# A two-layer hybrid trunk in fp32r: VectorE put in program order, weight tiles split two tiles ahead

## The chip, the cores and the metric

The kernel runs on one core of a Trainium2 chip. The metric is device microseconds of one execution. The kernel before took 2461.07 us (median of three runs, 2458.48 to 2471.07).

## The reference

Two decoder layers over 256 tokens of width 2048, in float32. Layer 0 mixes tokens with stick-breaking attention, layer 1 with an S5 state-space layer and a gated linear unit (GLU). After each mixer stands a dense MLP of width 8192.

```
cond = silu(c)
for i in range(2):
    sh1, sc1, g1, sh2, sc2, g2 = split(cond @ ada_w[i] + ada_b[i], 6)   # the conditioning vectors
    h = rmsnorm(x, ln1_g[i]) * (1 + sc1) + sh1
    y = stick_breaking_mixer(h) if i == 0 else s5_mixer(h)
    x = x + g1 * y
    h = rmsnorm(x, ln2_g[i]) * (1 + sc2) + sh2
    a = relu(h @ mlp_w1[i])
    x = x + g2 * ((a * a) @ mlp_w2[i])
```

`s5_mixer` is `u = h @ w_in`, a scan over time in 16 blocks of 128 channels, `z = gelu(y + d * u)`, and `(z @ w_glu)` cut in two halves `a * sigmoid(g)`.

## The kernel before

All weights stream from HBM, one pass: 736 weight tiles `w` of 512 KB (`weights`, L126). Each product is made of three matmuls on rounded halves, so each weight tile is rounded by ScalarE to `wh` (L131) and the rest `wl = w - wh` is made by VectorE (L133). `w`, `wh` and `wl` have three buffers each. TensorE then runs 24 matmuls of about 256 columns on a tile (L160 to L162, `cols_tile`), or 12 of 512 columns (L146 to L148, `gemm_rows`). The tiles come in this order: attention 0 to 127, first MLP 128 to 383, S5 input product 384 to 415, GLU 416 to 479, second MLP 480 to 735.

Beside them runs a second stream, the conditioning vectors. `ada_w` comes in 384 loads of 512 KB (`adaw`, four buffers, L268 and L270). From the first MLP on one such load is one product on VectorE (L354, L356) into one of three accumulators (`adsums`, two buffers, and `adacc`); after 16 loads an accumulator is full, and after 32 TensorE sums it over partitions (`totals`, L327). One call of `tick` stands behind each weight tile. It lets `pump` emit `rate` loads of this stream (1.0 for the first 16 tiles of the first MLP, 0.42 in the rest of it, 0.35 in S5), plays three recorded VectorE operations of S5's tables (`Recorder`, L35), and runs what was planned for this tick. In the GLU `pace(44, ...)` sets the rate so that the vectors `mid` are done by the sixth of its eight groups, where `drain` asks for them and `fold` makes the operands `hH`, `hL` of the second MLP.

What sets the order: TensorE and GpSimd run in the order of the program's text. VectorE, ScalarE and the queue of SyncE (SP), which issues nearly all loads, are ordered by a scheduler that takes what it believes to be ready, by priority. So a conditioning product could stand ahead of its place in the text, until all three accumulators were taken.

S5 in one block `bi` of 128 channels, by ticks: `s5_windows` (VectorE L1029, ScalarE L1030) makes `u` from the product; a tick later `s5_shuffle` (TensorE L1038) gathers `u` through the identity; a tick after that `s5_states` runs eight matmuls of L1053 per complex half and seven VectorE operations (L1055 to L1063); four ticks later `s5_outputs` (L1078, L1079) makes `y`. The next block's `s5_windows` is in the same tick as this block's `s5_states`, and stands behind it in the text.

Of the kernel before, what the change touches and what calls it, by code (L numbers as in the profile page):

```python
# [8 lines left out]
F32 = mybir.dt.float32  # L9
# [3 lines left out]
AF = mybir.ActivationFunctionType  # L13
OP = mybir.AluOpType
AX = mybir.AxisListType

P = 128
D = 2048
NB = D // P
# [37 lines left out]
class Trunk:  # L57
    def __init__(self, ctx, tc, ins, out, dbg=None):
        self.ctx, self.tc, self.nc = ctx, tc, tc.nc
        self.i, self.out, self.dbg = ins, out, dbg or {}  # L60
        self.pers = ctx.enter_context(tc.tile_pool(name="pers", bufs=1))
        self.wp = ctx.enter_context(tc.tile_pool(name="wp", bufs=1))
        self.ps = ctx.enter_context(tc.tile_pool(name="ps", bufs=1, space=bass.MemoryType.PSUM))
        self.queue = []
        self.acc2 = self.wp.tile([P, 2, 512], F32, name="adacc", bufs=1)


# [55 lines left out]
        self.nc.vector.tensor_tensor(lo, src, hi.bitcast(F32), op=OP.subtract)  # L123


    def weights(self, src, a, b):  # L126
        nc = self.nc
        w = self.wp.tile([P, a, b], F32, name="w", bufs=self.nw)
        nc.sync.dma_start(w, src)
        h = self.wp.tile([P, a, b], F32R, name="wh", bufs=self.nh)  # L130
        nc.scalar.activation(h, w, AF.Copy)  # L131
        l = self.wp.tile([P, a, b], F32R, name="wl", bufs=self.nh)
        nc.vector.tensor_tensor(l, w, h.bitcast(F32), op=OP.subtract)  # L133
        return h, l

    def gemm_rows(self, w2d, c0, aH, aL, k0, k1):
        nc = self.nc
        acc = self.accs()
        for t in range(k0 // 2, k1 // 2):
            r0 = 2 * t * P  # L140
            H, L = self.weights(w2d[r0:r0 + 2 * P, c0:c0 + 512].rearrange("(a p) b -> p a b", p=P), 2, 512)
            for kk in range(2):
                kb = 2 * t + kk
                for tb in range(2):
                    o, s = acc[:, tb], slice(tb * P, tb * P + P)
                    nc.tensor.matmul(o, aL(kb)[:, s], H[:, kk], start=(kb == k0), stop=False)  # L146
                    nc.tensor.matmul(o, aH(kb)[:, s], L[:, kk], start=False, stop=False)  # L147
                    nc.tensor.matmul(o, aH(kb)[:, s], H[:, kk], start=False, stop=(kb == k1 - 1))  # L148
            self.tick()
        return acc  # L150

    def cols_tile(self, acc, w2d, c0, t, aH, aL, k0=0, k1=NB):
        nc = self.nc
        r0, n = 4 * t * P, aH(0).shape[-1]
        H, L = self.weights(w2d[r0:r0 + 4 * P, c0:c0 + 256].rearrange("(a p) b -> p a b", p=P), 4, 256)
        for kk in range(4):
            kb = 4 * t + kk
            for j in range(2):
                o, s = acc[:, j, :n], slice(j * P, j * P + P)
                nc.tensor.matmul(o, L[:, kk, s], aH(kb), start=(kb == k0), stop=False)  # L160
                nc.tensor.matmul(o, H[:, kk, s], aL(kb), start=False, stop=False)  # L161
                nc.tensor.matmul(o, H[:, kk, s], aH(kb), start=False, stop=(kb == k1 - 1))  # L162
        self.tick()
# [155 lines left out]
    def ada_dve(self, layer, groups):  # L319
        nc = self.nc  # L320
        st, rows = {}, 32 * len(groups)

        def totals(i0, accs):
            if i0 == 0:
                st["bank"] = self.ada_bank()
            for i, acc in enumerate(accs, i0):
                nc.tensor.matmul(st["bank"][32 * i:32 * i + 32], self.ones[:, 0:32], acc, start=True, stop=True)  # L327

        def evict():
            st["sm"] = self.ada_sums(st["bank"], rows)  # L330

        def finish():
            p2 = self.mp()
            for b in range(4):
                nc.tensor.transpose(p2[:, b * P:b * P + rows], st["sm"][:rows, b * P:b * P + P], self.ident[:rows, :rows])
            src = p2.rearrange("p (b i r) -> p i r b", b=4, i=4)[:, :, 0]
            for i, (vec, g) in enumerate(groups):
                self.ada_done(layer, vec, 4 * g, 4, src[:, i])

        accs = []  # L340
        if self.sums is not None:
            for i in range(0, len(groups), 2):
                if self.turn % 3:
                    acc = self.sums.tile([P, 1024], F32, name="adsums", bufs=2)
                else:
                    acc = self.acc2.rearrange("p a b -> p (a b)")
                self.turn += 1
                accs += [acc[:, :512], acc[:, 512:]]
                vec, g = groups[i]
                for k in range(NB):  # L350
                    wt = self.ada_load(layer, vec, g, k, wide=True).rearrange("p a b -> p (a b)")
                    c = self.cond[:, k:k + 1]
                    if k == 0:
                        nc.vector.tensor_scalar(acc, wt, c, None, op0=OP.mult)  # L354
                    else:
                        nc.vector.scalar_tensor_tensor(acc, wt, c, acc, op0=OP.mult, op1=OP.add)  # L356
                    yield
            self.later(2, totals, 0, accs)
        for i, (vec, g) in enumerate(groups if not accs else []):
            acc = self.acc2[:, self.turn % 2]  # L360
            self.turn += 1
            accs.append(acc)
            for t in range(8):
                wt = self.ada_load(layer, vec, g, t)
                for kk in range(2):
                    c = self.cond[:, 2 * t + kk:2 * t + kk + 1]
                    if t + kk == 0:
                        nc.vector.tensor_scalar(acc, wt[:, kk], c, None, op0=OP.mult)
                    else:
                        nc.vector.scalar_tensor_tensor(acc, wt[:, kk], c, acc, op0=OP.mult, op1=OP.add)  # L370
                yield
            self.later(2, totals, i, accs[i:])
        self.later(2, evict)
        self.later(3, finish)

    def ada_vec(self, layer, vec, on_pe=False):
        g = self.pending[layer, vec] = self.ada(layer, [(vec, g) for g in range(4)], on_pe)
# [61 lines left out]
    def square(self, sq, kb):  # L439
        nc = self.nc  # L440
        if kb == 0:
            nc.scalar.activation(sq, self.xT[:, kb], AF.Square)
        else:
            t = self.wp.tile([P, S], F32, name="sqt", bufs=2)
            nc.scalar.activation(t, self.xT[:, kb], AF.Square)
            nc.vector.tensor_tensor(sq, sq, t, op=OP.add)

    def new_sq(self):
        return self.wp.tile([P, S], F32, name="sqa", bufs=1)
# [52 lines left out]
    def mlp(ctx, self, layer, nxt=None, last=False, between=None):  # L502
        nc = self.nc
        w1, w2 = self.i["mlp_w1"][layer], self.i["mlp_w2"][layer]
# [3 lines left out]
        sq = self.new_sq() if nxt else None  # L508
# [3 lines left out]
        for q in range(4):  # L512
            aH = rp.tile([P, NB, S], F32R, name="aH", bufs=1)
            aL = rp.tile([P, NB, S], F32R, name="aL", bufs=1)
            if q == 0:
# [3 lines left out]
                for g in range(ahead):  # L519
                    acc = self.gemm_cols(w1, g * 256, hH, hL, 0, 8)  # L520
# [4 lines left out]
            for g in range(8):  # L525
                if 8 * q + g < ahead:
                    acc = self.gemm_cols(w1, q * 2048 + g * 256, hH, hL, 8, 16)
                    r = src = halves[8 * q + g]
                    nc.vector.tensor_tensor(src, src, acc[:, :, :S + 1], op=OP.add)
                else:  # L530
                    src = self.gemm_cols(w1, q * 2048 + g * 256, hH, hL)
                    r = rp.tile([P, 2, S + 1], F32, name="rl")
                self.normal(r, src, AF.Relu)
                r = r[:, :, :S]
                nc.scalar.activation(r, r, AF.Square)
                self.split(aH[:, 2 * g:2 * g + 2], aL[:, 2 * g:2 * g + 2], r)
            if q == 3 and nxt:
                nxt()
                self.sq = sq
            if last:  # L540
                for g in range(4):
                    c = slice(g * 512, g * 512 + 512)
                    acc = self.gemm_rows(w2[q * 2048:q * 2048 + 2048], g * 512, lambda kb: aH[:, kb], lambda kb: aL[:, kb], 0, NB)
# [14 lines left out]
            for g in range(8):  # L558
                acc = self.gemm_cols(w2[q * 2048:q * 2048 + 2048], g * 256, lambda kb: aH[:, kb], lambda kb: aL[:, kb])[:, :, :S]
# [4 lines left out]
                if q == 1 and between:  # L564
                    nc.vector.tensor_tensor(halves[g], halves[g], acc, op=OP.add)
                    acc = halves[g]
# [616 lines left out]
    def run(self):  # L1183
        nc = self.nc
# [28 lines left out]
        self.modulate(0, 4)  # L1213
        self.attention(sets, gates[0])
        self.dump("x1")
        M = lambda i: bool(0 >> i & 1)
        self.sums = self.ctx.enter_context(self.tc.tile_pool(name="sums", bufs=1))
        mid = [self.ada_vec(1, 4, M(4)), self.ada_vec(1, 3, M(5))]
        nxt = [self.ada_vec(1, 1, M(1)), self.ada_vec(1, 0, M(2))]
# [64 lines left out]
```

## Time and profile before

| | |
|---|---|
| median of the runs | 2461.07 us |
| the profiled execution's own time | 2467.97 us |
| its span | 2466.1 us |
| TensorE matmul busy | 2365.1 us, 96% of the span |
| VectorE busy | 1795.4 us, 73% |
| ScalarE busy | 1212.7 us, 49% |
| moved by DMA | 627.09 MB, 254 GB/s over the span |
| mean granted TensorE clock | 0.989 |

Matmuls overlap, so their busy time hides part of what is lost between them; the count of matmuls in a stretch tells more. The shares are means over stages of different kinds, so the stretches in the rows below are cut along the stages: 572 to 1306 us is most of the first MLP, 1347 to 1498 us is S5, 1539 to 1673 us most of the GLU, and from 1719 us on the second MLP runs.

### The profile page before, as it was taken

To read this page: it belongs to the slowest core of one execution; us is meant where nothing else is said; L and a number is where in the kernel's file an instruction comes from. 1 tells how busy PE (TensorE), PEld (TensorE's weight loads), DVE (VectorE), ACT (ScalarE), POOL (GpSimd) and SP (SyncE) were. 2 spreads that over 40 slices of the span, in tenths; PEclk is the share of its full clock that TensorE was granted. 3 is DMA by queue.
4 is the path that set the end of the run, shared out by engine and by line. 5 is a ranking of instruction groups with operands and counts; after the bars stand their busy time and mean duration, and the time that the engine had idled before them with its cause. 6 is when DMAs were issued, how large, how long until landed. Compare 5 with 4: busy or idle time off the path is not lost.

```text
span 2466.1 us, 45235 instructions
## 1 busy us (share of the span) xinstructions
PE 2365.1 (96%) x18355; PEld 2160.4 (88%) x18355; DVE 1795.4 (73%) x2223; ACT 1212.7 (49%) x1814; POOL 316.6 (13%) x340
## 2 busy tenths in 40 slices
PE   7999999999998999889999999989999999999999
PEld 4777789899988899889998998989998998998987
DVE  5789999999778767875786668888744554555554
ACT  4534875346334335435546776434554543543543
POOL 0000110001056545445300000000000000000000
PEclk9999999999999999999999999999999999999999
DMA  9888899999999967997798544999856555556565
GB/s 341 302 299 306 288 308 320 322 303 294 310 310 315 300 207 230 309 299 219 259 316 276 174 154 159 314 329 314 281 175 192 184 186 190 175 179 193 180 195 164
DMA packets 416773, 627.09 MB, mean 254 GB/s; under 512 B 19858, under 2 KB 282420, under 8 KB 414260
## 3 DMA queue, kind: packets, MB, share of 16 engines
q1 hardware_dynamic: 411968, 606.16, 74.8%
q0 software_dynamic: 3968, 17.83, 2.2%
q8 instruction: 144, 2.36, 0.4%
q14 instruction: 65, 0.53, 0.1%
q10 hardware_dynamic: 628, 0.21, 0.0%
HBM read 607.34 MB, written 16.78 MB: 253 GB/s over the span
## 4 chain that ended last, share of the span: by engine, by line
PE 44%; DMA 6%; DVE 5%; issue 3%; ACT 0%; SPq 0%; DVEq 0%; ACTq 0%
PE acc L160 9%; PE acc L162 8%; PE acc L161 8%; DMA adaw<-in_ada_w 5%; PE acc L146 5%; PE acc L148 5%; PE acc L147 5%; DVE wl L133 2%; PE mp L1053 1%; DVE adsums L356 1%; PE mp L1078 1%; PE mp L1038 1%; PE mp L1015 1%; DVE xT L435 1%; DMA w<-in_s_w_glu 0%
## 5 line engine op out<-in xcount | busy, mean ns | idle before, releaser
L131 ACT ACTIVATE wh<-w 128x1024 fp32r<-128x1024 f32 x736 | 777.5, 1058 | 1030.9 <-PE acc L162 364.6
L133 DVE TENSOR_TENSOR wl<-w,wh 128x1024 fp32r<-128x1024 f32 x736 | 922.6, 1255 | 436.9 <-ACT wh L131 434.3
L160 PE MATMUL acc<-hH,wl 128*128 128x258 f32 (+1 forms) x2816 | 808.4, 287 | 28.4 <-DVE wl L133 26.1
L162 PE MATMUL acc<-hH,wh 128*128 128x258 f32 (+1 forms) x2816 | 799.2, 284 | 0.0
L161 PE MATMUL acc<-hL,wh 128*128 128x258 f32 (+1 forms) x2816 | 797.8, 283 | 0.2 <-DVE hL L123 0.2
L160 PEld LDWEIGHTS acc<-hH,wl 128*128 128x128 f32 x2816 | 535.8, 190 | 44.3 <-DVE wl L133 33.6
L161 PEld LDWEIGHTS acc<-hL,wh 128*128 128x128 f32 x2816 | 536.3, 190 | 0.6 <-DVE hL L123 0.4
L162 PEld LDWEIGHTS acc<-hH,wh 128*128 128x128 f32 x2816 | 534.8, 190 | 0.0
L160 PE MATMUL acc<-aH,wl 128*128 128x256 f32 x1024 | 294.3, 287 | 26.4 <-DVE wl L133 25.5
L161 PE MATMUL acc<-aL,wh 128*128 128x256 f32 x1024 | 289.5, 283 | 0.0
L162 PE MATMUL acc<-aH,wh 128*128 128x256 f32 x1024 | 289.4, 283 | 0.0
L356 DVE SCALAR_TENSOR_TENSOR adsums<-adaw,cond,adsums 128x1024 f32<-128x1024 f32 x150 | 199.1, 1328 | 53.6 <-DMA adaw<-in_ada_w 53.0
L160 PEld LDWEIGHTS acc<-aH,wl 128*128 128x128 f32 x1024 | 194.3, 190 | 34.1 <-DVE wl L133 33.7
L146 PE MATMUL acc<-wh,aL 128*128 128x512 f32 x512 | 202.2, 395 | 0.0
L148 PE MATMUL acc<-wh,aH 128*128 128x512 f32 x512 | 202.1, 395 | 0.0
L147 PE MATMUL acc<-wl,aH 128*128 128x512 f32 x512 | 202.0, 395 | 0.0
L161 PEld LDWEIGHTS acc<-aL,wh 128*128 128x128 f32 x1024 | 194.4, 190 | 0.0
L162 PEld LDWEIGHTS acc<-aH,wh 128*128 128x128 f32 x1024 | 194.2, 190 | 0.0
L370 DVE SCALAR_TENSOR_TENSOR adacc<-adaw,cond,adacc 128x512 f32<-128x512 f32 x240 | 179.2, 750 | 3.1 <-DMA adaw<-in_ada_w 1.3
L146 PE MATMUL acc<-wh,hL 128*128 128x512 f32 x384 | 157.5, 410 | 5.8 <-ACT wh L131 3.1
L147 PE MATMUL acc<-wl,hH 128*128 128x512 f32 x384 | 153.8, 401 | 3.3 <-DVE wl L133 3.2
L148 PE MATMUL acc<-wh,hH 128*128 128x512 f32 x384 | 152.9, 398 | 0.0
(311 smaller groups left out, 2751.0 us busy)
## 6 DMA issues: line engine op xcount, KB each, us to landing
w<-in_mlp_w SPq DMA_DIRECT2D x512, 512.0 KB, 4.0
adaw<-in_ada_w SPq DMA_DIRECT2D x384, 512.0 KB, 6.0
w<-in_sb_w_in SPq DMA_DIRECT2D x96, 512.0 KB, 5.2
w<-in_s_w_glu SPq DMA_DIRECT2D x64, 512.0 KB, 5.4
w<-in_sb_w_out SPq DMA_DIRECT2D x32, 512.0 KB, 5.7
w<-in_s_w_in SPq DMA_DIRECT2D x32, 512.0 KB, 4.8
pw<-W POOLq DMA_DIRECT2D x8, 1024.0 KB, 6.5
W<-pw SPq DMA_DIRECT2D x8, 1024.0 KB, 7.7
```

Source lines behind the costliest of these rows:

```text
L131: nc.scalar.activation(h, w, AF.Copy)
L133: nc.vector.tensor_tensor(l, w, h.bitcast(F32), op=OP.subtract)
L146: nc.tensor.matmul(o, aL(kb)[:, s], H[:, kk], start=(kb == k0), stop=False)
L147: nc.tensor.matmul(o, aH(kb)[:, s], L[:, kk], start=False, stop=False)
L148: nc.tensor.matmul(o, aH(kb)[:, s], H[:, kk], start=False, stop=(kb == k1 - 1))
L160: nc.tensor.matmul(o, L[:, kk, s], aH(kb), start=(kb == k0), stop=False)
L161: nc.tensor.matmul(o, H[:, kk, s], aL(kb), start=False, stop=False)
L162: nc.tensor.matmul(o, H[:, kk, s], aH(kb), start=False, stop=(kb == k1 - 1))
L356: nc.vector.scalar_tensor_tensor(acc, wt, c, acc, op0=OP.mult, op1=OP.add)
L370: nc.vector.scalar_tensor_tensor(acc, wt[:, kk], c, acc, op0=OP.mult, op1=OP.add)
L435: nc.vector.scalar_tensor_tensor(x, y, self.mod[layer][:, vec * 16 + kb:vec * 16 + kb + 1], x, op0=OP.mult, op1=OP.add)
L1015: nc.tensor.transpose(pe[:, q * P:q * P + P], E[:, c, q].rearrange("p j a e -> p (j a e)"), self.ident)
```

## The change

From the first MLP on VectorE is in program order too (`manual_schedule` with DVE). Four things in the text change with it:

- `weights` no longer loads and splits the tile that is asked for; it keeps three tiles ready. A generator lists the tiles in the order of use, and the load, the rounding and the split of tile t+2 stand ahead of the matmuls of tile t.
- A conditioning product is emitted when the load two places behind it has been emitted (`overdue(2)`), and all that are left ahead of `totals`.
- The split of the MLP's activations (`aL`) and the sum of squares are put off by one tick (`behind`).
- All else on VectorE keeps its place in the text, and so gets that place on the engine.

```diff
-        self.queue = []
+        self.queue, self.seq, self.ready, self.due = [], None, [], []
...
     def weights(self, src, a, b):
+        if self.seq is None:
+            return self.fetch(src, a, b)
+        while len(self.ready) < 3 and self.seq:
+            nxt, a_, b_ = self.seq.pop(0)
+            self.ready.append((str(nxt), self.fetch(nxt, a_, b_)))
+        name, pair = self.ready.pop(0)
+        assert name == str(src), (name, str(src))
+        return pair
+
+    def fetch(self, src, a, b):
+        src = src.rearrange("(a p) b -> p a b", p=P)
         nc = self.nc
         w = self.wp.tile([P, a, b], F32, name="w", bufs=self.nw)
         nc.sync.dma_start(w, src)
...
         def totals(i0, accs):
+            self.overdue(0)
...
-                    c = self.cond[:, k:k + 1]
-                    if k == 0:
-                        nc.vector.tensor_scalar(acc, wt, c, None, op0=OP.mult)
-                    else:
-                        nc.vector.scalar_tensor_tensor(acc, wt, c, acc, op0=OP.mult, op1=OP.add)
+                    self.due.append((self.ada_product, acc, wt, k))
+                    self.overdue(2)
...
+    def overdue(self, n):
+        while len(self.due) > n:
+            fn, *args = self.due.pop(0)
+            fn(*args)
...
-            nc.vector.tensor_tensor(sq, sq, t, op=OP.add)
+            self.behind(nc.vector.tensor_tensor, sq, sq, t, OP.add)
+
+    def behind(self, fn, *args):
+        if self.seq is None:
+            fn(*args)
+        else:
+            self.at(1, fn, *args)
...
-                self.split(aH[:, 2 * g:2 * g + 2], aL[:, 2 * g:2 * g + 2], r)
+                nc.scalar.activation(aH[:, 2 * g:2 * g + 2], r, AF.Copy)
+                self.behind(nc.vector.tensor_tensor, aL[:, 2 * g:2 * g + 2], r, aH[:, 2 * g:2 * g + 2].bitcast(F32), OP.subtract)
...
         self.dump("x1")
+        self.ctx.enter_context(self.tc.manual_schedule(engines={mybir.EngineType.PE, mybir.EngineType.Pool, mybir.EngineType.DVE}))
+        self.seq = list(self.tiles())
```

Place one is SP's queue in the first MLP, from weight tile 236 on (`w` a weight tile, `adaw` a conditioning load). The kernel before:

```order
L129 DMA w<-in_mlp_w 128x4x256 x2
L268 DMA adaw<-in_ada_w 128x1024
L129 DMA w<-in_mlp_w 128x4x256
L268 DMA adaw<-in_ada_w 128x1024
L129 DMA w<-in_mlp_w 128x4x256 x42
L268 DMA adaw<-in_ada_w 128x1024
L129 DMA w<-in_mlp_w 128x4x256
L268 DMA adaw<-in_ada_w 128x1024 x2
```

And the changed kernel in the same stage:

```order
L165 DMA w<-in_mlp_w 128x4x256 x2
L304 DMA adaw<-in_ada_w 128x1024
L165 DMA w<-in_mlp_w 128x4x256 x3
L304 DMA adaw<-in_ada_w 128x1024
L165 DMA w<-in_mlp_w 128x4x256 x2
L304 DMA adaw<-in_ada_w 128x1024
```

Before, conditioning loads come close together and then stop for 42 weight tiles; now one stands behind every two or three weight tiles all along.

Place two is SP's queue in the GLU, from about weight tile 424 on. The kernel before:

```order
L129 DMA w<-in_s_w_glu 128x4x256 x2
L268 DMA adaw<-in_ada_w 128x1024
L129 DMA w<-in_s_w_glu 128x4x256 x2
L268 DMA adaw<-in_ada_w 128x1024
L129 DMA w<-in_s_w_glu 128x4x256
L268 DMA adaw<-in_ada_w 128x1024
```

And the changed kernel:

```order
L304 DMA adaw<-in_ada_w 128x1024 x3
L165 DMA w<-in_s_w_glu 128x4x256 x2
L304 DMA adaw<-in_ada_w 128x1024 x2
L165 DMA w<-in_s_w_glu 128x4x256
L304 DMA adaw<-in_ada_w 128x1024 x2
L165 DMA w<-in_s_w_glu 128x4x256
```

Counted along the whole queue, from weight tile 424 to 464 there stood 45 conditioning loads before and there stand 62 now. Up to tile 424 there were 308 of them before and are 290 now, and up to tile 464 the counts meet, 353 and 352.

Place three is VectorE in S5, one block of 128 channels (`u` the window, `w` and `R` the state's products, `M` the scan's factors). The kernel before:

```order
L1079 SCALAR_TENSOR_TENSOR u_14061<-u_14061,colv,mp 128x4x64
L1055 TENSOR_TENSOR w_14863<-mp,T 128x512
L1056 TENSOR_TENSOR w_14864<-mp,T 128x512
L1029 TENSOR_TENSOR u_14061<-acc,rms 128x257
L1057 TENSOR_TENSOR R<-w_14863,w_14864 128x512
L1060 SCALAR_TENSOR_TENSOR R<-M_14064,R 128x512
L1061 TENSOR_TENSOR w_14863<-R,T 128x512
L1062 TENSOR_TENSOR w_14864<-R,T 128x512
L133 TENSOR_TENSOR wl<-w,wh 128x1024
L1063 TENSOR_TENSOR R<-w_14863,w_14864 128x512
```

And the changed kernel (L1132 was L1079, L1108 to L1116 were L1055 to L1063, L1082 was L1029):

```order
L1132 SCALAR_TENSOR_TENSOR u_14070<-u_14070,colv,mp 128x4x64
L1108 TENSOR_TENSOR w_14685<-mp,T 128x512
L1109 TENSOR_TENSOR w_14686<-mp,T 128x512
L1110 TENSOR_TENSOR R<-w_14685,w_14686 128x512
L1113 SCALAR_TENSOR_TENSOR R<-M_14073,R 128x512
L1114 TENSOR_TENSOR w_14685<-R,T 128x512
L1115 TENSOR_TENSOR w_14686<-R,T 128x512
L1116 TENSOR_TENSOR R<-w_14685,w_14686 128x512
L1082 TENSOR_TENSOR u_14070<-acc,rms 128x257
L169 TENSOR_TENSOR wl<-w,wh 128x1024
```

The window `u` stood behind the second of the seven state operations and stands behind the seventh now; so it does in 15 of the 16 blocks. TensorE's and GpSimd's order is the same in both kernels.

## Rows read from the trace of the kernel before

**Rows 1.** Busy time by stretch; columns as the first line says, (x) counts instructions.
```profile
core 0: us, PE busy (x) PEld busy (x) DVE busy (x) ACT busy (x) POOL busy (x), PEclk, DMA share, GB/s
572.00:870.00 298.00, 274.74 (x2195) 268.25 (x2194) 244.25 (x234) 129.58 (x161) 119.64 (x116) 0.98 0.91 303
870.00:960.00 90.00, 90.00 (x758) 90.00 (x757) 57.74 (x63) 40.82 (x49) 35.92 (x42) 1.00 0.69 208
960.00:1120.00 160.00, 145.93 (x1190) 141.54 (x1189) 128.53 (x126) 62.61 (x72) 86.45 (x82) 1.00 0.88 291
1120.00:1200.00 80.00, 80.00 (x670) 80.00 (x670) 49.06 (x47) 42.45 (x55) 40.44 (x44) 1.00 0.74 227
1200.00:1306.00 106.00, 103.81 (x863) 101.81 (x862) 92.98 (x113) 51.62 (x74) 0.00 (x0) 1.00 0.90 300
1347.00:1498.00 151.00, 150.47 (x2596) 138.35 (x2595) 104.33 (x144) 110.40 (x231) 0.00 (x0) 1.00 0.51 160
1539.00:1673.00 134.00, 122.10 (x988) 118.04 (x987) 113.35 (x131) 53.82 (x69) 0.00 (x0) 0.99 0.94 323
1560.00:1620.00 60.00, 55.28 (x456) 53.42 (x455) 52.18 (x66) 25.87 (x35) 0.00 (x0) 1.00 0.98 339
1740.00:1800.00 60.00, 60.00 (x504) 60.00 (x503) 44.57 (x42) 33.59 (x46) 0.00 (x0) 1.00 0.82 267
```

**Rows 2.** Who waited for whom, 572 to 1306 us: total us, times, longest.
```profile
ACT wh L131 <- DMA w<-in_mlp_w: 221.9, 108, 5.6
...
PEld acc L160 <- DVE wl L133: 50.3, 48, 3.4
PE acc L160 <- DVE wl L133: 38.6, 36, 3.2
```

**Rows 3.** DMA issues, 572 to 870 us: count, size, median us to landing.
```profile
w<-in_mlp_w SPq DMA_DIRECT2D x90, 512.0 KB, 5.4
adaw<-in_ada_w SPq DMA_DIRECT2D x67, 512.0 KB, 6.1
```

**Rows 4.** DMA issues, 870 to 960 us.
```profile
w<-in_mlp_w SPq DMA_DIRECT2D x31, 512.0 KB, 3.8
```

**Rows 5.** VectorE by line, 554 to 590 us: busy us, mean ns, idle before.
```profile
L133 DVE TENSOR_TENSOR wl<-w,wh 128x1024 fp32r<-128x1024 f32 x12 | 14.5, 1218 | 1.1 <-ACT wh L131 1.1
L356 DVE SCALAR_TENSOR_TENSOR adsums<-adaw,cond,adsums 128x1024 f32<-128x1024 f32 x7 | 9.0, 1281 | 1.4 <-DMA adaw<-in_ada_w 1.4
L497 DVE TENSOR_TENSOR half<-half,rms 128x514 f32<-128x514 f32 x6 | 4.1, 686 | 0.0
```

**Rows 6.** VectorE's table operations (L35), 494 to 620 us: busy us and count.
```profile
494.00:620.00 126.00, 17.46 (x76) 1.00 0.91 301
```

**Rows 7.** The folds (L484): shortest, median and longest ns.
```profile
L484 DVE SCALAR_TENSOR_TENSOR hL<-xT,mod,hH x48: 476/479/483, 433.7 to 1726.7; 128x256 fp32r<-128x256 f32 x48
```

**Rows 8.** One S5 block in order of time: start us, duration us.
```profile
1409.14 0.69 DVE L1055 TENSOR_TENSOR w<-mp,T 128x512 f32<-128x512 f32 x1 [0.66 <-PE mp L1053]
...
1410.35 0.42 DVE L1029 TENSOR_TENSOR u<-acc,rms 128x257 f32<-128x257 f32 x1
1410.68 0.68 DVE L1057 TENSOR_TENSOR R<-w,w 128x512 f32<-128x512 f32 x1
1410.80 0.51 ACT L1030 ACTIVATE u<-u 128x256 f32<-128x256 f32 x1 [1.42 <-DVE u L1029]
...
1413.55 1.13 PE L1038 MATMUL mp<-u,ident 128*32 128x65 f32 x32
1413.87 1.22 DVE L133 TENSOR_TENSOR wl<-w,wh 128x1024 fp32r<-128x1024 f32 x1
...
1415.00 0.68 DVE L1063 TENSOR_TENSOR R<-w,w 128x512 f32<-128x512 f32 x1
```

**Rows 9.** DMA of the GLU, 1539 to 1673 us: GB/s in 40 slices, then issues.
```profile
GB/s 285 311 278 304 285 208 221 350 221 380 359 268 391 329 304 373 382 374 353 377 357 295 359 367 360 376 368 379 375 376 379 378 248 162 320 251 270 235 363 357
...
adaw<-in_ada_w SPq DMA_DIRECT2D x41, 512.0 KB, 6.5
w<-in_s_w_glu SPq DMA_DIRECT2D x40, 512.0 KB, 5.9
```

More of the change, by code (lines that the diff above doesn't have):

```diff
@@ L123, in split, with tiles @@
         self.nc.vector.tensor_tensor(lo, src, hi.bitcast(F32), op=OP.subtract)
-    def weights(self, src, a, b):
+    def tiles(self):
+        i = self.i
+        rows = lambda w, c0, k0=0, k1=NB: [(w[2 * t * P:2 * t * P + 2 * P, c0:c0 + 512], 2, 512) for t in range(k0 // 2, k1 // 2)]
+        cols = lambda w, c0, k0=0, k1=NB: [(w[4 * t * P:4 * t * P + 4 * P, c0:c0 + 256], 4, 256) for t in range(k0 // 4, k1 // 4)]
+        for layer in range(2):
+            w1, w2 = i["mlp_w1"][layer], i["mlp_w2"][layer]
+            if layer:
+                w, v = i["s5_w_in"][0], i["s5_w_glu"][0]
+                for g in range(8):
+                    yield from cols(w, g * 256)
+                yield from cols(v, D, 0, 12) + cols(v, 0, 0, 12) + cols(v, D, 12) + cols(v, 0, 12)
+                for g in range(1, 8):
+                    yield from cols(v, D + g * 256) + cols(v, g * 256)
+            for q in range(4):
+                if q == 0 and layer == 0:
+                    for k in (0, 8):
+                        for g in range(8):
+                            yield from cols(w1, g * 256, k, k + 8)
+                else:
+                    for g in range(8):
+                        yield from cols(w1, q * 2048 + g * 256)
+                part = w2[q * 2048:q * 2048 + 2048]
+                for g in range(4 if layer else 8):
+                    yield from rows(part, g * 512) if layer else cols(part, g * 256)
+    def weights(self, src, a, b):
+        if self.seq is None:
[8 more added lines that the diff above has]
+        src = src.rearrange("(a p) b -> p a b", p=P)
         nc = self.nc
@@ L140, in gemm_rows @@
             r0 = 2 * t * P
-            H, L = self.weights(w2d[r0:r0 + 2 * P, c0:c0 + 512].rearrange("(a p) b -> p a b", p=P), 2, 512)
+            H, L = self.weights(w2d[r0:r0 + 2 * P, c0:c0 + 512], 2, 512)
             for kk in range(2):
@@ L154, in cols_tile @@
         r0, n = 4 * t * P, aH(0).shape[-1]
-        H, L = self.weights(w2d[r0:r0 + 4 * P, c0:c0 + 256].rearrange("(a p) b -> p a b", p=P), 4, 256)
+        H, L = self.weights(w2d[r0:r0 + 4 * P, c0:c0 + 256], 4, 256)
         for kk in range(4):
@@ L374, in ada_dve, with ada_product @@
         self.later(3, finish)
+    def ada_product(self, acc, wt, k):
+        c = self.cond[:, k:k + 1]
+        if k == 0:
+            self.nc.vector.tensor_scalar(acc, wt, c, None, op0=OP.mult)
+        else:
+            self.nc.vector.scalar_tensor_tensor(acc, wt, c, acc, op0=OP.mult, op1=OP.add)
+    def overdue(self, n):
+        while len(self.due) > n:
+            fn, *args = self.due.pop(0)
+            fn(*args)
     def ada_vec(self, layer, vec, on_pe=False):
@@ L445, in square @@
             nc.scalar.activation(t, self.xT[:, kb], AF.Square)
-            nc.vector.tensor_tensor(sq, sq, t, op=OP.add)
+            self.behind(nc.vector.tensor_tensor, sq, sq, t, OP.add)
+    def behind(self, fn, *args):
+        if self.seq is None:
+            fn(*args)
+        else:
+            self.at(1, fn, *args)
     def new_sq(self):
```

## The prediction

> **What bounds the kernel now.** I read the table of engines first: matmuls fill 96% of the span, so TensorE is the bound and the question is where it is starved. The table by stretch tells that. In the lulls of the conditioning stream the first MLP runs 758 matmuls in 90 us and 670 in 80 us, 0.119 us each, 2.86 us for a weight tile of 24. In the bursts it does not: the three stretches from 572, 960 and 1200 us hold 2195 + 1190 + 863 = 4248 matmuls in 298 + 160 + 106 = 564 us, where 4248 x 0.119 = 505.5 us would do [rows 1]. So 58.5 us are lost there. The waits say to what: TensorE waits for `wl`, 50.3 us on its weight loads and 38.6 us on its matmuls (the two overlap), and ScalarE waits for `w` to land [rows 2]. The DMA issues say why: a weight tile lands 5.4 us after its issue in a burst, beside 67 conditioning loads to 90 tiles, and 3.8 us in a lull [rows 3, 4]. In S5 TensorE is busy 150.47 of 151 us, with DMA at 0.51. In the GLU it is busy 122.1 of 134 us, with DMA at 0.94 and 323 GB/s [rows 1].
>
> **First MLP, the conditioning stream spread out.** VectorE's products can no longer run ahead of their place, so the buffers come free one by one and the loads stand at 0.42 per tile. 1.42 loads of 0.524 MB in 2.86 us are 260 GB/s. The second MLP shows 267 GB/s with TensorE busy 60.00 of 60 us [rows 1], so that pace starves nobody. All of the loss given back would be -58.5 us. The other end is -20: VectorE in order holds splits behind the last quarter's residuals and `behind` operations, which wait for TensorE, and each such wait longer than the two tiles' lead (5.7 us) starves it. I take the middle of the two waits for `wl`, 50.3 and 38.6: -45.
>
> **The S5 tables.** 76 operations of 17.46 us stood early, in 494 to 620 us [rows 6]; in order, 52 of them fall on tiles 144 to 160 (three or so a tick), 52 x 0.23 = 11.9 us. VectorE then has, for these 16 tiles, 16 splits of 1.22, 7 products (0.42 a tile) of 1.28, 24 operations on `half` of 0.69 [rows 5] and these: 19.5 + 9.0 + 16.5 + 11.9 = 56.9 us, against 16 x 2.86 = 45.8 us of TensorE. The lead takes some of the 11 us: +8. Tiles 128 to 144 get rid of the same work, where loads are the limit: -6. Together +2, between 0 and +12. The eight folds of 0.479 us [rows 7] that must now pass ahead of the next operands' splits: +2, between 0 and 4.
>
> **S5, the window behind the state operations.** In the block shown, VectorE made `u` at 1410.35, behind the second state operation; ScalarE had it at 1411.31, and TensorE's shuffle began at 1413.55, 2.2 us later [rows 8]. Now `u` stands behind the seventh. That one (L1063) began at 1415.00; without the window (0.33 to the next start) and the split (1.13 to the next start) ahead of it, it begins at 1413.54 and ends at 1414.2. The window then ends by 1414.6, ScalarE's copy by 1415.16, and the shuffle can begin at 1415.25, 1.7 us late. TensorE runs in order, so nothing passes the shuffle, and the stretch has no idle time to absorb it. Fifteen blocks: 15 x 1.7 = +25.5. Bounds: 0, if the state operations start earlier, and 15 x 2.5 = +37, if the split gets in ahead too. I take 25.5, as every start in it is from the one block's rows.
>
> At the end of S5 twelve splits of `z`, the shape of a fold, stand in a row on VectorE: 12 x 0.48 = 5.8 us before the last outputs. With TensorE's lead of 5.7 us against them and the states' operations: +4, between 0 and 8.
>
> **GLU, more loads in the same tiles.** Less of the stream is done by then, and `pace` must still finish by the sixth group: 62 conditioning loads stand between tiles 424 and 464 where 45 stood. With 40 tiles that is 102 loads, 53.5 MB. These tiles are the stretch of 134 us in [rows 1], with DMA at 0.94. Its fullest part, 1560 to 1620 us, moved 339 GB/s at 0.98. At 339 GB/s 53.5 MB take 157.8 us: +24. At the stretch's own 323 GB/s it would be 165.6 (+32). At 375 GB/s, about what the best slices reach [rows 9], 142.6 (+9). VectorE gets 17 more products, 113.35 + 17 x 1.28 = 135.1 us [rows 1, 5], so that below +1 it would be the bound itself. I take 339, the longest stretch with full queues: +24, between +1 and +32.
>
> In the sixth group ten folds (4.8 us, [rows 7]) and the residual stand in order ahead of splits, against 5.7 us of lead: +5, between 0 and 9.
>
> **No cost.** The second MLP gets the conditioning loads that are left, at a quarter load per tile, which is the 267 GB/s row again: 0. The order of TensorE and GpSimd is unchanged.
>
> **Sum.** -45 + 2 + 2 + 25.5 + 4 + 24 + 5 = +17.5 us. The profiled execution took 2467.97 us, so 2485.5; it lies 6.9 us above the median of the runs, 2461.07, so on the runs' basis 2478.6, called 2479.
>
> **Rivals.** *The GLU is not limited by loads* (the other side). Its 323 GB/s is then what was asked for, not what the queues give: before, buffers came free only as VectorE got to the products, and a strict order may feed them better. For it: slices of 376 to 382 GB/s [rows 9]. Against: a share of 0.94 to 0.98 at 323 to 339 GB/s [rows 1]. The price is 53.5 MB over the rate; the other terms sum to -6.5, so the point is a GLU of 140.5 us, 381 GB/s, below which the kernel is not slower, and with the floor of +1 and the full -58.5 in the first MLP it comes to 2461.1 - 6.5 - 13.5 + 1 = 2442. At 375 GB/s with -58.5 it is 2450.
>
> The Trainium skill, "DMA: Bandwidth & Descriptors", section "Measured (HBM→SBUF, 128 partitions, SWDGE, issued from GpSimd)", speaks for this rival: it has 425 GB/s for a lone core at 16 MB. By that the GLU's loads would take 126 us (an estimate from that page), and loads would not bound it. No stretch of this trace comes near; the fullest is the 339 GB/s used above, so the trace does not bear the page out for this mix of loads.
>
> *The window's lateness is hidden.* If the state operations of a block get done earlier, because no split or product stands between them, the shuffle finds `u` ready: 2478.6 - 25.5 = 2453. For it: in the old order a split and the window stood among the seven. Against: both are already taken out in the working above, and 1.7 us are still missing.
>
> *The strict order starves TensorE in the first MLP in new places.* A split behind an operation that waits for TensorE's own result makes a cycle of waits in each group, and only 10 of the 58.5 us come back: 2478.6 + 35 = 2514. For it: VectorE is busy 244 of 298 us in the burst stretch [rows 1], with little room to catch up. Against: two tiles of lead.
>
> *The stream isn't spread.* If loads still came in clumps, the first MLP would stay as it is, and the GLU with it. The new queue has one load behind every two or three tiles, so this is almost excluded.
>
> **How the numbers follow.** What a measurement of this kernel can tell from no change is about 0.5%, 12.3 us: below 2448.8 is faster, above 2473.4 slower. The forecast has 0.50 (its own range 2458 to 2500: slower 0.36, same 0.11, faster 0.03). The GLU's rival has 0.20 (2442 to 2461: faster 0.11, same 0.08, slower 0.01), the hidden window 0.13 (faster 0.05, same 0.06, slower 0.02), the starved MLP 0.14 (slower 0.13, same 0.01), no spreading 0.03 (same 0.02, faster 0.01). That makes slower 0.52, same 0.28, faster 0.20. The range of 8 in 10 leaves out the low tail of the GLU's rival and the high one of the starved MLP: 2440 to 2512.
>
> **What would show it.** Right: the first MLP has no stretch with more than 0.122 us per matmul behind tile 160, and waits for `wl` nearly vanish there; in S5 the shuffle waits for ScalarE's `u` in each block, and a block takes some 1.7 us more; tiles 424 to 464 take some 158 us with DMA at 0.98. Wrong: a GLU above 360 GB/s, no wait ahead of the shuffle, waits for `wl` in the first MLP that stay above 25 us, or TensorE starved in the second MLP, which I cost at nothing.

## The result, and the profile after

The changed kernel took 2571.4 us, median of four runs (2568.51 to 2574.55), against 2462.55 us before: a ratio of 1.0438, 95% interval 1.0405 to 1.0470. It is slower, as forecast, but by 109 us where 17.5 were forecast, and it lies outside the range of 2440 to 2512.

From the time at which TensorE starts each weight tile the loss can be put to stages. The first row gives the time between two tiles in the profile of before, the rows below it how much more (+) or less (-) each kernel took; below the changed kernel stand the experiments of the next section. Each row comes from one profiled execution. Attention, tiles 0 to 127, is the same program in all of them and came out 0 to 4.3 us shorter than in this profile of before: a difference of a few us in one cell can be spread.

| tiles | 0-144 | 144-160 | 160-384 | 384-416 | 416-424 | 424-464 | 464-480 | 480-735 | sum |
|---|---|---|---|---|---|---|---|---|---|
| stage | | first MLP, start | first MLP | S5 | entry of GLU | GLU | GLU, end | second MLP | |
| before, us | 511.9 | 46.9 | 710.6 | 191.7 | 40.7 | 133.7 | 46.9 | 737.7 | |
| changed kernel | -4.3 | +16.8 | -15.5 | +39.0 | +12.1 | +50.1 | +5.4 | +2.8 | +106 |
| e5 VectorE free | -6.8 | +2.6 | +2.7 | +0.6 | +0.3 | -2.7 | +2.7 | +2.7 | +2 |
| e1 window first | -3.9 | +17.2 | -19.4 | -2.2 | +17.7 | +47.1 | +5.4 | +2.3 | +64 |
| e2 fewer GLU loads | -5.1 | +20.5 | -5.7 | +38.1 | +2.8 | +11.8 | +5.4 | +2.7 | +71 |
| e3 split one ahead | -3.1 | +17.3 | +40.5 | +36.6 | +13.1 | +20.3 | +13.7 | +27.1 | +166 |
| e4 totals later | -5.4 | +18.3 | -16.1 | +38.7 | +6.8 | +34.1 | +6.2 | +0.4 | +83 |
| e6 tables, one a tick | -4.3 | +9.8 | -7.1 | +39.0 | +12.1 | +46.6 | +5.4 | +2.7 | +104 |
| e7 products at loads | -6.6 | +16.1 | -32.6 | +36.2 | +7.4 | +11.0 | +5.5 | +0.3 | +37 |
| d1 products one behind | -5.9 | +16.7 | -31.1 | +38.6 | +5.7 | +29.1 | +5.5 | +1.4 | +60 |
| c2 e1, e2, e4, e6 | -6.3 | +16.9 | +3.0 | -0.8 | +7.1 | +2.3 | +5.3 | -0.5 | +27 |
| c3 e1, e7 | -6.7 | +17.5 | -33.9 | -2.2 | +14.4 | +9.6 | +5.4 | +0.0 | +4 |
| c4 three edits | -3.5 | +10.6 | -28.0 | -1.5 | +14.2 | +9.8 | +5.3 | -0.6 | +6 |
| c5 loads in S5 | -4.3 | +11.8 | -28.3 | -0.5 | +9.8 | -8.3 | +5.3 | -0.4 | -15 |
| c6 loads in first MLP | -7.9 | +16.1 | -21.2 | +0.8 | +7.4 | -6.4 | +5.5 | +0.4 | -5 |
| c8 statistics later | -7.7 | +10.9 | -27.2 | -2.4 | +10.1 | -9.2 | +6.3 | -4.9 | -24 |

Busy time by stretch in the changed kernel, cut at tiles 144, 160, 384, 416, 424 and 464; the columns are those of [rows 1].

```profile
544.60:608.30 63.70, 50.41 (x386) 48.08 (x385) 53.04 (x96) 31.54 (x45) 0.00 (x0) 0.97 0.64 208
608.30:1303.40 695.10, 670.04 (x5476) 658.34 (x5477) 529.17 (x551) 311.14 (x383) 286.26 (x282) 0.99 0.82 266
1303.40:1534.10 230.70, 196.18 (x2936) 181.25 (x2934) 141.80 (x186) 136.74 (x292) 5.12 (x11) 0.94 0.53 172
1534.10:1586.90 52.80, 44.27 (x657) 39.54 (x653) 41.13 (x55) 18.65 (x33) 0.00 (x0) 0.89 0.54 180
1586.90:1770.70 183.80, 143.76 (x985) 133.96 (x986) 130.20 (x135) 53.79 (x68) 0.00 (x0) 0.87 0.88 286
```

In the GLU (the last line) the core moved 286 GB/s, less than the 323 GB/s of [rows 1], although it had more to load. VectorE was busy 130 of 184 us and TensorE got a granted clock of 0.87. No engine is full there and the queues are not either, so something waits in a circle. The chain of waits shows one turn of it. In the changed kernel a weight tile is loaded in L165, rounded in L167 and split in L169; a conditioning load is L304, its product L415; SPq is the queue of SP (start us, duration, what):

```profile
1597.13 7.34 DMA w<-in_s_w_glu
...
1604.57 1.06 ACT wh L167
...
1605.66 0.12 DVE wl L169
1605.78 1.02 issue
1606.80 1.29 DVE adacc L415
1608.09 0.02 issue
1608.11 0.33 SPq L304
1608.44 0.06 issue
1608.50 0.42 SPq L165
...
1609.02 7.15 DMA w<-in_s_w_glu
```

A weight tile lands, is rounded and split (the split fills the 1.02 us called issue too), and only then VectorE gets to a conditioning product. The product's load has landed by then: over tiles 424 to 464 products waited 0.7 us in all for a landing, where they waited 12.1 us before. That product frees a buffer, so SP's queue can issue the next conditioning load, and only behind it stands the next weight load, which takes another 7 us. One turn is 11.9 us. SP's own waits over tiles 424 to 464 (total us, times, longest), the changed kernel:

```profile
SPq L304 <- DVE adsums L415: 65.2, 28, 5.4
SPq L304 <- DVE adacc L415: 38.8, 20, 4.8
SPq L165 <- DVE wl L169: 25.5, 9, 6.4
```

and the kernel before in the same tiles:

```profile
SPq L129 <- DVE wl L133: 49.6, 24, 4.4
SPq L268 <- DVE adacc L356: 11.5, 10, 2.3
SPq L268 <- DVE adsums L356: 11.4, 8, 3.1
```

Waits of SP for a product went from 22.9 to 104.0 us. VectorE's wait at a split for the rounded tile, and TensorE's for the split, in the changed kernel and then in the kernel before:

```profile
DVE wl L169 <- ACT wh L167: 43.6, 24, 3.9
PE acc L196 <- DVE wl L169: 33.1, 15, 4.4
```

```profile
DVE wl L133 <- ACT wh L131: 6.3, 9, 2.5
PE acc L160 <- DVE wl L133: 10.4, 8, 2.6
```

In the scheduler's order VectorE lost 6.3 us at splits whose tile wasn't there; in program order it loses 43.6, and the products behind those splits stand still with it.

In S5 one block of the changed kernel reads so (start, duration, engine, line; in brackets the wait):

```profile
1426.55 0.69 DVE L1116 TENSOR_TENSOR R<-w,w 128x512 f32<-128x512 f32 x1
...
1427.15 0.42 DVE L1082 TENSOR_TENSOR u<-acc,rms 128x257 f32<-128x257 f32 x1
...
1427.81 0.52 ACT L1083 ACTIVATE u<-u 128x256 f32<-128x256 f32 x1
...
1428.37 1.13 PE L1091 MATMUL mp<-u,ident 128*32 128x65 f32 x32 [1.99 <-ACT u L1083]
...
1429.43 0.42 PE L196 MATMUL acc<-hH,wl 128*128 128x258 f32 x1
```

This is the wait of the forecast: the window behind the seventh state operation, ScalarE, and a shuffle that starts 2.0 us late (1.7 were worked out from [rows 8]). It stands in all 15 blocks, 13 times with 2.0 to 2.2 us and in the last two with 4.1 and 3.3. The last falls into the entry of the GLU; the other 14, over tiles 384 to 416, are

```profile
PE mp L1091 <- ACT u L1083: 30.0, 14, 4.1
```

Behind the wait shown the matmuls of the product take 0.42 us where they took 0.28 before it, and the granted clock from 1428.4 to 1432.0 us is 0.67. So it is behind 7 of the 14 waits; behind the other 7, as behind the one of the block before (third line), it stays at 1.00:

```profile
1423.00:1426.00 3.00, 3.00 (x38) 2.67 (x37) 2.90 (x5) 0.78 (x2) 0.00 (x0) 1.00 0.80 319
1428.40:1432.00 3.60, 3.60 (x44) 3.39 (x45) 2.64 (x3) 1.85 (x5) 0.00 (x0) 0.67 0.64 200
1414.10:1417.70 3.60, 3.60 (x53) 3.38 (x54) 2.64 (x3) 1.85 (x5) 0.00 (x0) 1.00 0.63 211
```

In the first MLP TensorE waits less for `wl` than before, but at a place where it did not wait at all: the sums over partitions (L364) stand still for the late products. Matmuls' waits over tiles 160 to 384:

```profile
PE acc L196 <- DVE wl L169: 16.1, 16, 2.6
PE mp L364 <- DVE adsums L415: 6.7, 2, 3.6
PE mp L364 <- DVE adacc L415: 2.1, 1, 2.1
```

and in the kernel before, where this is the only such line:

```profile
PE acc L160 <- DVE wl L133: 38.5, 35, 3.2
```

### The profile page after: what moved, and what is told of

Its sections match the earlier page's. It is cut to its first block, busy times and chain, and to the rows that moved or that the text cites. A ratio compares the mean times of both kernels' runs of the same rounds, so it can differ in the third digit from the quotient of the medians.

```text
span 2572.5 us, 45168 instructions
## 1 busy us (share of the span) xinstructions
PE 2404.9 (93%) x18355; PEld 2191.8 (85%) x18355; DVE 1812.0 (70%) x2223; ACT 1211.4 (47%) x1814; POOL 320.2 (12%) x340
## 5 line engine op out<-in xcount | busy, mean ns | idle before, releaser
L167 ACT ACTIVATE wh<-w 128x1024 fp32r<-128x1024 f32 x736 | 777.8, 1058 | 1104.3 <-PE acc L198 391.4
L169 DVE TENSOR_TENSOR wl<-w,wh 128x1024 fp32r<-128x1024 f32 x736 | 926.5, 1263 | 475.9 <-ACT wh L167 474.7
L196 PE MATMUL acc<-hH,wl 128*128 128x258 f32 (+1 forms) x2816 | 825.3, 293 | 49.5 <-DVE wl L169 47.7
L197 PE MATMUL acc<-hL,wh 128*128 128x258 f32 (+1 forms) x2816 | 813.2, 289 | 4.6 <-DVE hL L536 4.5
L198 PE MATMUL acc<-hH,wh 128*128 128x258 f32 (+1 forms) x2816 | 813.3, 289 | 0.0
L196 PEld LDWEIGHTS acc<-hH,wl 128*128 128x128 f32 x2816 | 552.1, 196 | 68.0 <-DVE wl L169 53.3
L197 PEld LDWEIGHTS acc<-hL,wh 128*128 128x128 f32 x2816 | 553.1, 196 | 5.1 <-ACT wh L167 4.7
L198 PEld LDWEIGHTS acc<-hH,wh 128*128 128x128 f32 x2816 | 551.0, 196 | 0.0
L415 DVE SCALAR_TENSOR_TENSOR adsums<-adaw,cond,adsums 128x1024 f32<-128x1024 f32 x150 | 198.9, 1326 | 0.8 <-DMA adaw<-in_ada_w 0.3
```

The lines of the kernel that those rows point to most:

```text
L415: self.nc.vector.scalar_tensor_tensor(acc, wt, c, acc, op0=OP.mult, op1=OP.add)
```

## Experiments

All are the changed kernel with an edit. Where no number of runs is given, the time is that of a single run. Executions of the kernel before lay between 2456 and 2474 us beside them, so a difference of 10 us between two single runs shows little by itself.

**e5, VectorE given back to the scheduler.**

```diff
-        self.ctx.enter_context(self.tc.manual_schedule(engines={mybir.EngineType.PE, mybir.EngineType.Pool, mybir.EngineType.DVE}))
+        self.ctx.enter_context(self.tc.manual_schedule(engines={mybir.EngineType.PE, mybir.EngineType.Pool}))
```

> The changed kernel with VectorE given back to the scheduler; tiles fetched two ahead, delayed products and operations put off by a tick stay. If the strict order alone costs the 109 us, this is within 1% of 2462 us (2440 to 2485), S5 loses its 2.0 us stall per block and the GLU's tiles 424 to 464 go from 184 back to some 135 us. If the early fetch or the delayed products are to blame, it stays above 2530.

2466.61 us (ten runs), ratio to before 1.0008 (0.9993 to 1.0023). Without the strict order the whole cost is gone: it lies in that order, with the positions that the text gives it here, and fetching two tiles ahead costs and gains nothing under the scheduler. The bursts of conditioning loads are back too (again 42 weight tiles without one), and with them the old first MLP (160 to 384: +2.7).

**e1, the window ahead of the state operations.**

```diff
                 self.at(t, self.s5_windows, bi, acc[:, b])
+                p = self.plan[self.now + t]
+                p.insert(next((i for i, x in enumerate(p) if x[0] == self.s5_states), len(p) - 1), p.pop())
```

> The changed kernel with S5's window emitted ahead of the state operations of the same tick. If the late window is what S5 lost, the 15 stalls of 2.0 us at the shuffle and the slow TensorE stretch behind each go: tiles 392 to 415 take some 140 us as before, not 171, and the kernel 2530 (36 to 42 us less than 2571); the GLU stays as slow as in the changed kernel. If something else in S5's order holds it, it stays above 2555.

2532.3 us. In the plan of one tick the window now stands ahead of the state operations. S5 goes from +39.0 to -2.2 us, with all its other operations in strict order, and no shuffle waits for `u` over tiles 384 to 416, so the one position was the whole loss there. The GLU stays at +47.1: the two losses are separate. The entry of the GLU loses 5.6 us more, for one sum over partitions waits 8.9 us there where it waited 3.9.

**e2, fewer loads in the GLU.** 0.50 conditioning loads per tile in the first MLP, not 0.42. While TensorE runs tiles 424 to 464, 43 such loads are issued, where the changed kernel issues 59 and the kernel before 41. (The 62 and 46 of the expectations count along the queue's order; the counts below are of issues in this stretch of time.)

```diff
-            self.rate = 0.42
+            self.rate = 0.5
```

> The changed kernel with 0.50 conditioning loads per tile in the first MLP, so that 46 of them and not 62 stand between tiles 424 and 464 (45 before the change). If the number of loads is what the GLU pays for, these tiles go from 184 to 135 to 145 us and the kernel to 2530. If the strict order of splits and products is (each waits for the other's load, one after the other), they stay at 160 us or more, since the order is the same with fewer links, and the kernel gains 10 to 25 us at most.

2538.37 us, tiles 424 to 464 in 145.5 us: by its expectation this speaks for the number of loads, at the edge of what it named. The entry of the GLU falls to +2.8, and the first MLP loses 10 us by it.

**e3, load two ahead, split one ahead.**

```diff
+        for r in self.ready[:2]:
+            if len(r[1]) == 3:
+                r[1] = self.rest(*r[1])
...
```

`rest` makes the split `wl = w - wh`, here for tiles t and t+1.

> The changed kernel with load and rounding two tiles ahead but VectorE's split one tile ahead, so that the split stands behind the products of one more tick; all 62 loads stay in the GLU. If the strict order is what starves the GLU (products that free buffers stand behind a split that waits for its tile), tiles 424 to 464 go from 184 to 150 to 160 us and the kernel to about 2540. If it is the number of bytes, they stay above 175.

The whole went the other way, to 2633.92 us, which the expectation missed: one tile's lead is too little in the MLPs. From 610 to 1361 us TensorE waits for the split again (total us, times, longest):

```profile
PEld acc L202 <- DVE wl L175: 74.6, 51, 3.4
PE acc L202 <- DVE wl L175: 68.4, 43, 3.2
```

But tiles 424 to 464 took 154.0 us with 58 conditioning loads, at 341 GB/s:

```profile
1643.30:1797.30 154.00, 130.63 (x984) 121.78 (x985) 128.18 (x134) 53.84 (x68) 0.00 (x0) 0.97 0.99 341
```

So the bytes alone don't take 184 us, and the reading of e2 was too simple. The two act together: each conditioning load adds a link to the circle, and either fewer links or a looser order opens it.

**e4, sums over partitions a tick later than their products.**

```diff
-            self.later(2, totals, 0, accs)
+            self.later(1, self.overdue, 0)
+            self.later(3, totals, 0, accs)
...
```

The last products before a sum are emitted a tick earlier too, and what reads the sums moves along with them.

> The changed kernel with the last delayed products emitted one tick earlier and the totals one tick later, so that TensorE's sums over partitions stand two ticks behind their products on VectorE and not in the same tick. If TensorE's stalls at the sums (7 + 2 us in the first MLP, 11 us in the GLU, 3 us at the transposes behind them, and the slow TensorE behind each) come from that, they vanish and the kernel takes 2545 (20 to 30 us less). If the sums only wait where the weight tiles would make TensorE wait anyway, it stays above 2560.

2551.09 us. The first MLP gains nothing, against the expectation: TensorE no longer waits at the sums there, but its matmuls' waits for `wl` go from 16.1 to

```profile
PE acc L196 <- DVE wl L169: 25.4, 26, 3.6
```

The wait has moved. The GLU and its entry gain 21 us (+50.1 to +34.1, and +12.1 to +6.8). There the sums did stop TensorE, up to 4.1 us at a time.

**e6, one table operation per tick.**

```diff
-            self.recorder.play(6 if self.early else 3)
+            self.recorder.play(6 if self.early else 1)
```

> The changed kernel with one operation of S5's tables per tick and not three. If the tables are what costs 17 us between tiles 144 and 160, these lose less than 4 us, and the 76 operations go by unseen until tile 220: the kernel takes 2555 to 2560. If the loads of the first 24 tiles or the folds are the cause, the 17 us stay.

2572.66 us, no gain, where 2555 to 2560 was expected. Tiles 144 to 160 recover 7.0 of 16.8 us. Two operations per tick recover as much (c4 below against c3, 17.5 to 10.6), so the tables seem to be less than half of that loss. The remaining tables were played in a row from 647 to 660 us, ahead of a split, and the weight tile behind it took 11.4 us where it takes 2.85.

**e7, each product at its own load.** The changed kernel's products are emitted two loads late; this one has no lateness.

```diff
-                    self.overdue(2)
+                    self.overdue(0)
```

> The changed kernel with each conditioning product at its own load, not two loads behind. If a late product costs buffers (two of the four are held by loads whose product is not yet emitted, so SP's queue and the weight load behind it wait), SP waits less for VectorE's products, the GLU's tiles 424 to 464 take 155 us or less, not 184, and the sums' stalls shrink too: 2530. If VectorE in order has to wait for the landing of a load just issued, and the splits behind it too, the first MLP loses 20 us and more and the kernel takes above 2590.

2507.7 us, 64 less than the changed kernel. Tiles 424 to 464 take 144.7 us with 55 conditioning loads, and the first MLP gains 17 us more. Stretch and SP's waits in the GLU:

```profile
1561.50:1706.20 144.70, 125.79 (x986) 118.50 (x985) 126.33 (x132) 53.81 (x68) 0.00 (x0) 0.99 0.99 348
```

```profile
SPq L304 <- DVE adsums L415: 44.2, 27, 3.4
SPq L165 <- DVE wl L169: 29.3, 17, 4.0
SPq L304 <- DVE adacc L415: 22.2, 18, 2.4
```

Waits for products fall from 104.0 to 66.4 us, the core moves 348 GB/s at a share of 0.99, and TensorE's clock is back at 0.99. VectorE waits 15.9 us at splits, not 43.6. With the product at its load VectorE stands in the order in which the loads were issued. In the first MLP (tiles 160 to 384) the waits at the sums are gone and those for `wl` are as long as in the changed kernel:

```profile
PE acc L196 <- DVE wl L169: 16.3, 20, 2.0
```

So late products cost the first MLP its 17 us by way of the sums: some 15 of the 17 stand in the tiles at which TensorE waited for them (197, 274 and 350) and the tiles right behind. That a held buffer is the reason in the GLU wasn't tried by itself: no run gave the conditioning loads more than their four buffers.

**d1, one load behind.**

```diff
-                    self.overdue(2)
+                    self.overdue(1)
```

> The changed kernel with conditioning products one load behind, between the changed kernel (two behind: GLU tiles 424 to 464 take 184 us, whole 2571) and products at their loads (145 us, 2508). If each load of lateness holds one of the four buffers and so shortens SP's run ahead, this lies between: 155 to 172 us, whole 2525 to 2550. If only the last step into SP's way matters, it equals one of the two ends within 5 us.

2528.02 us. Tiles 424 to 464 take 162.8 us with 58 conditioning loads, between 183.8 (two behind, 59) and 144.7 (none, 55): each load of lateness costs about 20 us there, less some us for the loads that were issued before the stretch. In the first MLP it is no scale: one behind is as good as none (-31.1 and -32.6 us), two gives -15.5.

**c2, c3, c4: edits together.** c2 has e1, e2, e4 and e6. c3 has e1 and e7; c4 has two table operations per tick besides.

> The changed kernel with the window first, 0.50 loads per tile, the sums a tick later and one table operation per tick. If the four causes are separate, the gains add: 42 (window) + 33 (loads) + 25 (sums) + 14 (tables) = 114 us, so 2457, level with the kernel before. If the gains overlap (a stall taken away turns up at the next wait), it stays above 2480.

> The changed kernel with the window first and the products at their loads. The gains lie in different stages, so they should add: 2571 - 39 - 64 = 2468, level with the kernel before (2455 to 2480). If the S5 stalls gave SP time to load ahead for the GLU, the GLU loses again what S5 gains, and it stays above 2485.

> As the kernel with window first and products at their loads, and with two operations of S5's tables per tick, not three. At one per tick tiles 144 to 160 lost 9.8 and not 16.8 us, but the rest was played in a row at the end and gave 8.5 us back; at two almost none is left over. 3 to 7 us less than with three: 2461 to 2465, no different from the kernel before within 0.5%; the 20 us gained in the first MLP are spent at the entry of the GLU.

c2 took 2497.09 us, above what it expected: the gains overlap, and the faster rate and the tables took the first MLP from -15.5 to +3.0. c3 took 2475.22 us (four runs; 1.0049, 1.0031 to 1.0067), c4 2474.42 us (six runs; 1.0043, 1.0029 to 1.0056); c3 came out 7 us above its 2468, within its range, and c4 9 us above its range. In c4 the first MLP from tile 160 on and S5 are 29 us ahead of the kernel before, and tiles 416 to 464 lose 24 again.

**c5, c6: c4 with some of the GLU's loads taken elsewhere**, into S5 (c5) or the first MLP (c6). In tiles 424 to 464 45 conditioning loads are issued in both, in c4 55.

c5:

```diff
-        self.rate = 0.35
+        self.rate = 0.8
```

c6:

```diff
-            self.rate = 0.42
+            self.rate = 0.48
```

> Window first, products at their loads, tables two a tick (2474 us), and 0.8 conditioning loads per tile in S5 in place of 0.35, so that 48 and not 62 stand between tiles 424 and 464. If the rest of the GLU's loss is the number of loads, tiles 416 to 464 lose 8 us or less, not 24, S5 pays nothing (its DMA was half idle), and the kernel takes 2457 to 2461, at or under the one before. If 14 more products on VectorE make the window or the outputs of S5 late, S5 loses 10 us and more and nothing is gained.

> As before with S5 at its old 0.35 loads per tile and the first MLP at 0.48 in place of 0.42: again 48 loads between tiles 424 and 464. If the number of loads is what is left, tiles 416 to 464 lose 8 us or less as with the loads in S5; the first MLP, at 0.48 with its weights at 0.52 MB in 2.86 us (271 GB/s), loses under 5 us of the 21 it gains: 2460 to 2465. If the strict order is what is left, the GLU's loss stays at 20 us or more in both runs.

c5 took 2456.52 us (eight runs; 0.9953, 0.9935 to 0.9972), c6 2468.4 us (ten runs; 1.0005, 0.9991 to 1.0019), 3 us above its range. Tiles 424 to 464 go from +9.8 to -8.3 and -6.4 us: that part of the loss was the number of loads, as forecast. S5 carries the loads for 1 us, the first MLP pays 7 and its start 5. The entry, tiles 416 to 424, stays at +7 to +10 in both. With 45 loads and no lateness the stretch takes 125.4 us, with 43 late ones (e2) 145.5: lateness costs some 20 us there, and more with the changed kernel's 59. (c5 and e2 also differ in S5 and in the tables.)

**c8, c5 with the statistics' matmul one tick later.**

```diff
-        self.at(1, self.rms_stat, self.sq)
-        self.at(3, self.rms_rows)
+        self.at(2, self.rms_stat, self.sq)
+        self.at(4, self.rms_rows)
```

The edit stands in two places, the MLP and S5.

> As with the 14 loads in S5 (2457), and the matmul on the sum of squares one tick later (it waits 4.1 us ahead of S5 and 4.5 us ahead of the second MLP), as are the rows made from it. If the putting off by a tick is what makes it wait, both waits fall under 1.5 us and the kernel takes 2448 to 2454. If the wait only moves to the operations that need the rows, the time stays within 2 us of 2457.

2444.14 us (six runs), ratio 0.9933 (0.9913 to 0.9953), below both kernels and 4 us below its range, with VectorE still in program order. Against c5's 0.9953 the intervals touch, so what this last edit gains is not well known. The wait it aims at, in c5 and then in c8:

```profile
PE mp L507 <- DVE sqa L107: 8.5, 2, 4.3
```

```profile
PE mp L507 <- DVE sqa L107: 2.6, 2, 1.5
```

The profiles of c8 and c5 lie 9 us apart, the two waits 5.9; 3.4 us of the 9 lie in tiles 0 to 127, which no edit touches, and are spread.

## Why the prediction was wrong

The direction held, and so did the two causes it led with, S5's window and the GLU. Their sizes, and the gain set against them, did not.

- **First MLP, -45 forecast, -15.5 measured (tiles 160 to 384).** The step that failed is -45 itself: it took the waits for `wl` as given back nearly whole ("that pace starves nobody"), and had no term for the products two behind. In undisturbed parts the pitch is the forecast one, 2.85 us a tile (tiles 178 to 181), and waits for `wl` more than halved: 19.4 and 16.1 us from 608 to 1303 us, where [rows 2] has 50.3 and 38.6. But they didn't vanish, and late products cost 17 us here (e7), 8.8 of them as waits of TensorE at the sums. Even e7's -32.6 falls short of -45; matmuls still wait 16.3 us for `wl` in it, and why those splits are late wasn't tried. The rival of a starved MLP, 10 us given back, came nearer in its number than the forecast for this stage.
- **Tables and folds, +8 and +2 forecast for tiles 144 to 160, +16.8 measured; -6 forecast for tiles 128 to 144, -3.5 measured.** VectorE's load was estimated about right (56.9 us for 53.0 measured), but the lead of two tiles absorbed none of the excess. e6 takes 7.0 off. One wait of 4.5 us is for the folds' `hL`, a term put at +2, and waits of 6.9 us are for `wl`; what makes the rest of the loss is open.
- **S5, +25.5 forecast, +39.0 measured.** The mechanism was right and e1 shows it. The term was mis-sized: 30.0 us of waits over 14 blocks, 2.0 us in most and 4.1 in one, instead of 1.7 each; and a granted clock that falls behind 7 of the 14 waits (0.94 over these tiles, 0.99 before), which the sum didn't have. The rival of a hidden window is refuted.
- **Entry of the GLU, +4 forecast, +12.1 measured.** Here a sum over partitions waits 3.9 us for late products (e4, without that wait: +6.8), and the last block's shuffle 3.3 us; neither was in the term. The term itself, the splits of `z`, shows in c4 and c5, where TensorE waits 6.4 and 5.0 us for S5's outputs `hH` and `hL`. The clock, 0.89 where it was 1.00, is part of the rest. What stays at +7 to +14 in e4 and c2 to c8 was not taken apart by a run.
- **GLU, +24 forecast, +50.1 measured.** The forecast set the price of bytes at 339 GB/s, 157.8 us. Without lateness the stretch takes 144.7 us (e7), +11. Of the remaining 39 us some 6 are four conditioning loads that e7 issues before the stretch (an estimate, 4 x 0.524 MB at 348 GB/s). The other 33 are the circle of split, product, conditioning load and weight load, for which the forecast had no term: it looked at VectorE's busy time and at the rate of the DMA, both of which had room, and not at what stands behind what in SP's queue while a split waits. The rival that loads don't limit the GLU was half right: the queues gave 348 GB/s where the order let them, above the 339 of the forecast. But its end, a kernel that isn't slower, did not come, as the strict order fed the queues worse and not better; and with the products at their loads the queues are full (a share of 0.99) and fewer loads gain 18 us (c5), so loads do limit this stage then.
- **End of the GLU, +5 forecast, +5.4 measured; second MLP 0 forecast, +2.8 measured.** As forecast in size; that the ten folds make the +5.4 was not tried.

Taken together the sum was 89 us too low: 29.5 in the first MLP, 9 in its first 32 tiles, 13.5 in S5, 8 at the entry, 26 in the GLU and 3 in the second MLP.

## What to carry to other kernels

When an engine goes into program order, write down for each pair of loads that share a queue what must have run on that engine before the next issue: a waiting operation now holds back the ones that free buffers, and through them the queue. In program order a consumer belongs at the place of its load, in the order of issue: here each load of delay cost some 20 us in the stage whose transfers were full, though one cost nothing in the first MLP. Place the work that another engine waits for (here the window) first within its tick, and move spare loads into the stage whose transfers are half idle. Program order itself need not cost anything: c8 keeps it.

## What the runs showed of the hardware

TensorE can pay twice for a wait. From 1631.8 us, behind a wait of 4.0 us for `wl`, one tile of 24 matmuls ran at a granted clock of 0.50, the 1.2 GHz level, and took 5.2 us; the second tile behind it, at 1.00, took 2.9, of which the second line shows 2.7. Not every wait has this price: of S5's 14 waits 7 had it, though 13 of the 14 were about equally long.

```profile
1631.80:1637.00 5.20, 5.20 (x24) 5.20 (x25) 3.30 (x3) 1.06 (x1) 0.00 (x0) 0.50 0.98 309
1640.30:1643.00 2.70, 2.70 (x25) 2.70 (x23) 2.37 (x3) 1.06 (x1) 0.00 (x0) 1.00 0.78 225
```

And the loads of this mix went faster than the fullest stretch of [rows 1] suggested, 339 GB/s: 348 GB/s over 144.7 us in e7 and, over 125.4 us in c5, 356 at a DMA share of 1.01:

```profile
1527.40:1652.80 125.40, 119.91 (x986) 116.18 (x985) 110.99 (x121) 53.62 (x68) 0.00 (x0) 1.00 1.01 356
```
